# Expert queries, choosing and fetches laid out head by head, with memory work moved among the fetches

## The chip, the core and the metric

The kernel runs on one core of a Trainium2 chip, in one launch. The metric is the device time of one execution in microseconds (us). Engines: PE multiplies matrices (PEld is its weight load), DVE and ACT work on vectors, POOL issues the indirect DMAs that fetch expert rows, SP issues the weight loads.

## What is computed

256 tokens of width 1024 in float32 go through a first mixer (differential attention and retention), a layer of product-key experts, a second mixer (state space and latent attention), an attention over a memory of 256 rows, and a feed-forward layer. The change touches the first two and the memory's keys and values. The expert layer, cut from the reference:

```python
q = (xb @ w_query).reshape(tb, PEER_HEADS, 2, PEER_KEY_DIM // 2)
s = jnp.einsum('thpd,hpnd->thpn', q, sub_keys).astype(jnp.float32)
top_s, top_i = lax.top_k(s, PEER_TOPK)
cand_s = (top_s[:, :, 0, :, None] + top_s[:, :, 1, None, :]).reshape(tb, PEER_HEADS, PEER_TOPK * PEER_TOPK)
...
best_s, pos = lax.top_k(cand_s, PEER_TOPK)
eid = jnp.take_along_axis(cand_i, pos, axis=-1)
gate = jax.nn.softmax(best_s, axis=-1)
u = jnp.take(expert_down, eid, axis=0)
act = jax.nn.gelu(jnp.einsum('thkd,td->thk', u, xb).astype(jnp.float32), approximate=False)
v = jnp.take(expert_up, eid, axis=0)
return jnp.einsum('thk,thkd->td', (gate * act).astype(v.dtype), v)
```

Each token has 8 heads; a head scores 128 keys in each of two halves, takes 16 of each, adds them in pairs, takes the 16 best pairs and so 16 of 16384 experts. For each expert a row of 2048 numbers is fetched: 1024 for a dot product with the token, 1024 that are added to its result with the weight gate times Gelu of the dot.

## The kernel before, in words

A matmul of full precision is made of three (lines 171 to 175): each operand is split into a rounded part and a rest. A piece of weights (line 148, 512 KB) is loaded by SP (`raw`, line 166), rounded by ACT (`wh`, line 167), and its rest taken by DVE (`wl`, line 168); each of the three has three buffers. The framework puts the instructions into each engine's queue from the dependences and a cost of its own, so an engine's order isn't quite that of the program; on an engine they run in that order.

**First mixer.** `mix1` computes six column blocks of `w_in`; three of them (`rqk`, `rv`, `rg`) and then the memory's values and keys are a generator of small steps, `fill`, that is called between the steps of the attentions so that PE has work while DVE and ACT compute softmaxes. The memory has 16 steps (`memory_values`, line 864): eight pieces of `w_mem_v`, with 12 matmuls of 128x512 each, and eight blocks of `w_mem_k`, with 24 of 128x256. Before the change nine of them (eight and one) run in `mix1`. Its results go to DRAM (`memkv`).

**Experts.** Tokens are two tiles of 128. `queries` (line 608) makes 16 blocks of queries, two for each head, and after every fourth block scores two heads of both tiles (line 629) and copies them (line 631). `extract` (line 588) takes the best 16 of a half's 128 scores by five DVE instructions (MAX8, FIND_INDEX8, MATCH_REPLACE8, MAX8, FIND_INDEX8; lines 593 to 605). `choose` (line 634) forms the pairs of the halves, extracts, makes gates, and finds the expert numbers by comparisons and sums (lines 677 to 683) into `eid` (line 685), for four heads at a time. So there are four units of picking: two tiles by two groups of four heads. The first unit ends before the first fetch; the others are laced among the first fetches of tile 0 by `picking`, a generator with a time debt (line 724).

The fetch loop (lines 753 to 794) goes over the 128 expert places of a tile in pairs. A place is an indirect DMA of 1 MB issued by POOL (line 767) into one of eight buffers `uv`, and a dot on DVE (`junk`, line 770). A pair has a Gelu on ACT (line 773), two diagonal tiles on DVE (`dg`, line 779) that carry the weights, and four times two matmul halves on PE (line 783), after which the two buffers are free. The rest of the memory's steps and the picking stand between the pairs of tile 0. After a tile, `joined` (line 816) adds the result to the residual and begins the next mixer's input; its product `xg` (line 828) runs on POOL, in the queue among the fetches of tile 1. The last pieces before the bridge are the latent weights `w_latq`.

The functions that the change touches:

Of the kernel before, what the change touches and what calls it, by code (L numbers as in the profile page):

```python
# [8 lines left out]
F32 = mybir.dt.float32  # L9
# [105 lines left out]
class K:  # L115
# [156 lines left out]
    def proj_N(self, xT, srcs, n, outs, ks=2, k0=0, start=True, stop=True, between=None, mid=None):  # L272
        last = len(srcs) - 1
        for i, s in enumerate(srcs):
            w = self.piece(s, [ks, n], None if i else between)
# [33 lines left out]
    def mix1(self):  # L309
# [3 lines left out]
        with self.tc.tile_pool(name="m1", bufs=1, reuse_waits="tile") as mp:  # L313
# [19 lines left out]
            def block(name):  # L333
                col = {"dq": 0, "dk": 512, "dv": 1024, "rqk": 1536, "rv": 2048, "rg": 2560}[name]
                o = [self.pa([128, 512]) for _ in range(2)]
                for i, _ in enumerate(self.proj_N(hT, [self.rows(I["w_in"], k * 256, 256, col, 512) for k in range(4)], 512, o,
                                     between=(lambda: load_xT(1, 1)) if name == "dq" else None)):
# [3 lines left out]
                if name == "dq":  # L341
                    yield
# [4 lines left out]
                if name == "rg":  # L347
                    gate = nc.scalar.activation(N[name], N[name], AF.Silu)
                    with self.tc.issue_after(gate.ins):
                        self.waves()  # L350
                elif q:
# [146 lines left out]
            fill(2)  # L498
            a = diff_turn(p)
            p = diff_scores(2)  # L500
            w = ret_scores(0)
            fill(2)
            run(norm)
            diff_out(1, a)
# [4 lines left out]
            p = diff_scores(3)  # L509
            fill(2)  # L510
            diff_out(2, a)
            ret_out(1, w)
            w = ret_scores(2)
            fill(2)
            a = diff_turn(p)
            ret_out(2, w)
            w = ret_scores(3)
            fill(1)
            diff_out(3, a)
            ret_out(3, w)  # L520
            ds = ds.rearrange("p t h -> p (t h)")
            nc.vector.tensor_scalar(ds, ds, 1.0 / 128, EPS, op0=OP.mult, op1=OP.add)
            r = self.rsqrt(ds, 8)
            for t in range(2):
# [3 lines left out]
            fill(2)  # L528
            self.to_T([blk(h) for h in range(4)], [dg] * 4, mT[0], mT[1], 0)
            fill(2)  # L530
# [19 lines left out]
            run(half(0, 0))  # L550
            run(half(1, 0))
            self.to_T([blk(4 + h) for h in range(4)], [self.pv("ret_g", h) for h in range(4)], mT[0], mT[1], 4)
            fill(1)
            run(half(0, 4))
# [5 lines left out]
            self.memory = fill  # L560
# [47 lines left out]
    def queries(self, pool, skT, sS):  # L608
# [4 lines left out]
        for b in range(16):  # L613
            if b < 2:
                o = two[b]
            else:
                o = self.pa([128, 256])
                self.proj_T(self.hT, self.piece(I["w_query"][b], [8, 128]), 8, o)
            if b == 2:
                self.r = self.res_r()  # L620
            if b % 4 == 0:
# [1025 lines left out]
```

## Time and profile before

| what | value |
|---|---|
| median of 3 runs | 1355.66 us (1355.19 to 1363.32) |
| the profiled execution | 1354.52 us, span of the profile 1352.6 us |
| busy share PE, PEld, DVE, ACT, POOL | 86, 59, 74, 36, 22% |
| fetched by indirect DMA | 268.45 MB, all DMA 388.07 MB |
| first and last fetch issued | 203.91 and 866.04 us |

The profile is of one execution; its times are from the span's start. A timeline row has start, duration, engine, line, operation, output<-input, and in brackets the idle time before it with the instruction that ended it. A group row has the count, the busy time and mean duration of one, and idle time of the engine before them with what ended it. A window row has the stretch's length, the busy time of each engine with its instructions, the granted TensorE clock as a part of full speed, the busy share of the 16 DMA engines and what they moved.

### The profile page before, as it was taken

Reading aid. Unit: us, or ns where it says so; the run is one execution under the profiler, and the core shown is the slowest. Engines: PE = TensorE matmul, PEld = TensorE weight load, DVE = VectorE, ACT = ScalarE, POOL = GpSimd, SP = SyncE. Lnnn points to the kernel's source line nnn. Section 1 sums busy time; section 2 is a strip of 40 time slices with the busy share of each in tenths; the row PEclk is TensorE's granted clock in tenths of the full one; section 3 lists DMA queues with packets and bytes.
Section 4 is the critical chain, followed back from the end, with each engine's and each line's share of the span. In section 5 each row is a group of like instructions: output and inputs, shape, how many; then the busy total and the mean of one; then the engine's idle time right before and its main releaser. Section 6 shows DMA issues by size and latency. Waiting matters only on the chain.

```text
span 1352.6 us, 16359 instructions
## 1 busy us (share of the span) xinstructions
PE 1158.9 (86%) x5430; PEld 792.1 (59%) x5430; DVE 997.2 (74%) x2334; ACT 489.1 (36%) x969; POOL 291.2 (22%) x280
## 2 busy tenths in 40 slices
PE   8999997668777777787777777789999999999996
PEld 6888996323223222332232222269997898999996
DVE  6877798997666666666656666678996886988887
ACT  6676653210000000100000000056878574755554
POOL 0010104335333334344343343210001000000001
PEclk9999998879999999999999999999999999999999
DMA  7636749899999999899999999936434364556562
GB/s 262 232 120 203 225 150 382 359 352 386 422 422 421 422 421 422 342 423 421 421 421 423 421 422 421 395 101 190 141 106 129 112 231 126 190 187 188 187 185 96
DMA packets 81655, 388.07 MB, mean 287 GB/s; under 512 B 8292, under 2 KB 10404, under 8 KB 48548
## 3 DMA queue, kind: packets, MB, share of 16 engines
q0 software_dynamic: 36864, 268.45, 48.2%
q1 hardware_dynamic: 42692, 115.96, 26.7%
q10 hardware_dynamic: 2016, 2.62, 0.5%
q8 instruction: 43, 0.70, 0.2%
q14 instruction: 40, 0.33, 0.1%
HBM read 383.86 MB, written 3.15 MB: 286 GB/s over the span
## 4 chain that ended last, share of the span: by engine, by line
PE 41%; DMA 23%; issue 13%; DVE 10%; POOL 6%; ACT 1%; POOLq 0%; DVEq 0%; ACTq 0%
DMA uv<-in_uv_dram,eid 23%; POOL uv L767 6%; PE pa L173 6%; PE pa L174 6%; PE pa L175 6%; PE pa L1476 4%; PE pb L173 4%; PE pb L174 4%; PE pb L175 4%; DVE junk L770 2%; DVE wl L168 1%; PE pb L783 1%; PE pb L1060 1%; DVE dg L779 1%; DVE eq L677 1%
## 5 line engine op out<-in xcount | busy, mean ns | idle before, releaser
L783 PE MATMUL pb<-uv,dg 128*128 128x512 f32 x1024 | 486.6, 620 | 168.5 <-DVE dg L779 160.0
L783 PEld LDWEIGHTS pb<-uv,dg 128*128 128x128 f32 x1024 | 190.3, 195 | 460.9 <-DVE dg L779 257.2
L770 DVE SCALAR_TENSOR_TENSOR junk<-uv,xn 128x1024 bf16<-128x1024 f32 x256 | 313.4, 1224 | 166.2 <-DMA uv<-in_uv_dram,eid 159.6
L767 POOL DMA_INDIRECT uv<-in_uv_dram,eid x256 | 260.4, 1017 | 431.7 <-PE pb L783 327.7
L168 DVE TENSOR_TENSOR wl<-raw,wh 128x1024 fp32r<-128x1024 f32 (+3 forms) x203 | 248.8, 1228 | 70.7 <-ACT wh L167 66.8
L167 ACT ACTIVATE wh<-raw 128x1024 fp32r<-128x1024 f32 (+3 forms) x203 | 212.1, 1047 | 196.5 <-PE pa L174 39.5
L773 ACT ACTIVATE dots<-dots,rs_y 128x2 f32<-128x2 f32 x128 | 37.8, 295 | 578.5 <-DVE junk L770 578.1
L173 PE MATMUL pb<-nTh,wh 128*128 128x256 f32 x416 | 117.7, 283 | 0.0
L174 PE MATMUL pb<-nTl,wh 128*128 128x256 f32 x416 | 117.7, 283 | 0.0
L175 PE MATMUL pb<-nTh,wl 128*128 128x256 f32 x416 | 117.4, 283 | 0.0
L779 DVE TENSOR_SCALAR dg<-cvt,dots,gate 128x128 f32<-128x128 f32 x256 | 78.0, 394 | 51.5 <-ACT dots L773 51.5
L174 PEld LDWEIGHTS pb<-nTl,wh 128*128 128x128 f32 x416 | 79.5, 191 | 1.0
L173 PEld LDWEIGHTS pb<-nTh,wh 128*128 128x128 f32 x416 | 79.5, 191 | 1.0
L175 PEld LDWEIGHTS pb<-nTh,wl 128*128 128x128 f32 x416 | 79.5, 191 | 0.0
L173 PE MATMUL pa<-nTh,wh 128*128 128x256 f32 x256 | 74.1, 289 | 0.0
L1500 POOL TENSOR_TENSOR xs<-xr,ng 128x512 f32<-128x512 f32 x4 | 5.1, 1294 | 313.9 <-DVE xr L1498 313.9
L175 PE MATMUL pa<-nTh,wl 128*128 128x256 f32 x256 | 72.5, 283 | 0.0
L174 PE MATMUL pa<-nTl,wh 128*128 128x256 f32 x256 | 72.4, 283 | 0.0
L173 PE MATMUL pa<-wh,nTh 128*128 128x512 f32 (+1 forms) x144 | 58.1, 412 | 8.2 <-ACT wh L167 7.1
L174 PE MATMUL pa<-wl,nTh 128*128 128x512 f32 (+1 forms) x144 | 57.6, 400 | 1.7 <-DVE wl L168 1.6
L175 PE MATMUL pa<-wh,nTl 128*128 128x512 f32 (+1 forms) x144 | 56.7, 394 | 0.0
L173 PEld LDWEIGHTS pa<-nTh,wh 128*128 128x128 f32 x256 | 48.9, 191 | 1.1 <-issue 1.0
(455 smaller groups left out, 1797.5 us busy)
## 6 DMA issues: line engine op xcount, KB each, us to landing
raw<-in_w_ffn_up_dram SPq DMA_DIRECT2D x44, 512.0 KB, 3.6
raw<-in_w_out_dram SPq DMA_DIRECT2D x24, 512.0 KB, 3.7
raw<-in_w_in_dram SPq DMA_DIRECT2D x23, 512.0 KB, 4.7
raw<-in_w_ffn_down_dram SPq DMA_DIRECT2D x22, 512.0 KB, 3.6
raw<-in_w_query_dram SPq DMA_DIRECT2D x16, 512.0 KB, 3.6
raw<-in_w_xbc_dram SPq DMA_DIRECT2D x16, 512.0 KB, 4.3
raw<-in_w_mem_v_dram SPq DMA_DIRECT2D x8, 512.0 KB, 4.7
raw<-in_w_mem_k_dram SPq DMA_DIRECT2D x8, 512.0 KB, 6.2
```

The lines of the kernel that those rows point to most:

```text
L167: nc.scalar.activation(h[:, s], raw[:, s], AF.Copy)
L168: self.wl = nc.vector.tensor_sub(lo[:, s], raw[:, s], h[:, s])
L173: mm(out, a[0], b[0], start=start, stop=False)
L174: mm(out, a[0], b[1], start=False, stop=False)
L175: mm(out, a[1], b[0], start=False, stop=stop)
L677: nc.vector.tensor_tensor(eq, ab[:, s, :, :, None].to_broadcast([128, H, 16, 16]), io, op=OP.is_equal)
L767: nc.gpsimd.indirect_dma_start(x, None, I["uv"], bass.IndirectOffsetOnAxis(ap=eids[:, s + i:s + i + 1], axis=0))
L770: nc.vector.scalar_tensor_tensor(junk, x[:, :1024], 1.0, xn[t], op0=OP.mult, op1=OP.mult, accum_out=dots[:, i:i + 1])
L773: nc.scalar.activation(dots, dots, AF.Gelu, scale=self.r[:, t:t + 1])
L779: nc.vector.tensor_scalar(dg[:, i], self.ident, ds[:, i:i + 1], gates[:, s0 + i:s0 + i + 1], op0=OP.mult, op1=OP.mult)
L783: nc.tensor.matmul(acc[d], dg[:, i], rs[i][:, 1024 + 512 * d:1536 + 512 * d], start=s0 + i == 0, stop=s0 + i == 127)
L1476: nc.tensor.matmul(acc[d][t], a[x][:, t * 128:(t + 1) * 128], w[y][:, d], start=b == 0 and x + y == 0, stop=b == 21 and x == 1)
```

## The change

1. `mix1` has no memory steps among its fillers any more, only the 12 steps of three `w_in` blocks. The order of attention and retention steps is changed, the block `rg` asks for its pieces one ahead, the gate's Silu and the angles come after the differential part, and the memory's normalization is laced into the output projection.
2. Queries are made head by head: two blocks, then that head's scores for both tiles.
3. Picking has seven units instead of four: of tile 0 head 0, head 1, heads 2 and 3, 4 and 5, 6 and 7; of tile 1 two of four heads. `choose` takes the first head and the count.
4. Fetching of tile 0 starts when head 0 is picked. The other query blocks, the picking and all 16 memory steps are laced among the fetches of both tiles.
5. The normalized tokens `xn` are formed by DVE in place of POOL, and the buffers `uv` no longer share space with the keys `skT`.

The diff, cut to its core:

```diff
             def fillers():
                 for name in ("rqk", "rv", "rg"):
                     yield from block(name)
-                yield from self.memory_values(*memory)
             fill = Filler(fillers())
...
             self.show("x1", xr)
-            self.memory = fill
+            self.memory = Filler(self.memory_values(*memory))
...
-        for b in range(16):
...
+        self.r = self.res_r()
+        for h in range(8):
+            qT = pool.tile([128, 2, 256], F32, name="qT", tag="qT", bufs=2)
+            for i in range(2):
+                o = two[i]
+                if h:
+                    o = self.pa([128, 256])
+                    self.proj_T(self.hT, self.piece(I["w_query"][2 * h + i], [8, 128]), 8, o)
+                nc.scalar.activation(qT[:, i], o, AF.Copy)
+                if h and not i:
+                    yield
+            for t in range(2):
+                s = self.pb([128, 2, 128])
...
+                nc.scalar.activation(sS[t][h], s, AF.Copy, scale=self.r[:, t:t + 1])
             yield
...
-            pick = [picks(t, hf) for t in range(2) for hf in range(2)]
+            units = [(0, 0, 1), (0, 1, 1)] + [(0, h, 2) for h in (2, 4, 6)] + [(1, 0, 4), (1, 4, 4)]
+            pick = [(u, picks(*u)) for u in units]
...
+                query = Filler(self.queries(qp, skT, sS))
+                query(4)
+                n = 4
+                picking(1e6, 0, 1)
+                nc.vector.tensor_mul(xn[0], xn[0], self.xr[:, 0])
+                acc = two()
+                tile0 = fetch(0, acc)
+                for s in tile0:
+                    if s in (2, 6, 10) or s > 10 and s % 6 == 4:
+                        query(1)
+                        n += 1
+                    picking(1400, 0, min(8, (n + 1) // 2))
+                    if s in (12, 28):
+                        picking(1e6, 0, 2 if s == 12 else 4)
+                    if n >= 15:
+                        break
+                query.rest()
...
+                for s in tile0:
+                    if s % 6 == 4:
+                        self.memory(1)
+                    picking(1400, 1, 8)
+                    if s in (60, 92):
+                        picking(1e6, 0, 6 if s == 60 else 8)
+                nc.vector.tensor_mul(xn[1], xn[1], self.xr[:, 1])
+                picking(1e6, 1, 4)
...
+                for s in fetch(1, acc):
+                    picking(1400, 1, 8)
+                    if s == 60:
+                        picking(1e6, 1, 8)
+                    if s % 6 == 4 and s < 100:
+                        self.memory(1)
+                    if s == 100:
                         self.memory.rest()
```

What the engines' queues then hold, at three places. `nTh` and `nTl` are the parts of the normalized input of the queries, `memTh` and `memTl` those of the memory, `uv` the fetched rows.

PE, around the first pair of expert matmuls, before:

```order
L175 MATMUL pa<-memTh,wl 128x256
L173 MATMUL pa<-memTh,wh 128x256
L174 MATMUL pa<-memTl,wh 128x256
L175 MATMUL pa<-memTh,wl 128x256
L173 MATMUL pa<-memTh,wh 128x256
L783 MATMUL pb<-uv,dg 128x512 x4
L174 MATMUL pa<-memTl,wh 128x256
L175 MATMUL pa<-memTh,wl 128x256
L173 MATMUL pa<-memTh,wh 128x256
L174 MATMUL pa<-memTl,wh 128x256
L175 MATMUL pa<-memTh,wl 128x256
```

The same place after:

```order
L173 MATMUL pa<-nTh,wh 128x256
L174 MATMUL pa<-nTl,wh 128x256
L175 MATMUL pa<-nTh,wl 128x256
L173 MATMUL pa<-nTh,wh 128x256
L174 MATMUL pa<-nTl,wh 128x256
L175 MATMUL pa<-nTh,wl 128x256
L769 MATMUL pb<-uv,dg 128x512 x4
L629 MATMUL pb<-skT,qT 128x128 x4
L769 MATMUL pb<-uv,dg 128x512 x4
L629 MATMUL pb<-skT,qT 128x128 x4
```

Before, all 16 query blocks and five memory-key blocks stand ahead of the first pair, and the memory's eight value pieces and first key block far ahead of those, in `mix1`. After, 11 query blocks and part of a twelfth stand ahead of it and no memory work; the remaining query blocks, the value pieces and three key blocks follow among the pairs up to the 23rd.

DVE, around the last expert numbers of tile 1 (the last picking of all), before:

```order
L679 TENSOR_TENSOR eq<-eq,rix 128x1024
L779 TENSOR_SCALAR dg<-cvt,dots,gate_1557 128x128 x2
L681 TENSOR_TENSOR eq<-eq 128x64x8
L682 TENSOR_TENSOR eq<-eq 128x64x4
L683 TENSOR_REDUCE rij<-eq 128x64
L770 SCALAR_TENSOR_TENSOR junk,dots<-uv,xn_1569 128x1024
L685 SCALAR_TENSOR_TENSOR eid_1560<-rij 128x64
L770 SCALAR_TENSOR_TENSOR junk,dots<-uv,xn_1569 128x1024
L779 TENSOR_SCALAR dg<-cvt,dots,gate_1557 128x128 x2
L770 SCALAR_TENSOR_TENSOR junk,dots<-uv,xn_1569 128x1024 x2
L779 TENSOR_SCALAR dg<-cvt,dots,gate_1557 128x128 x2
L770 SCALAR_TENSOR_TENSOR junk,dots<-uv,xn_1569 128x1024 x2
```

The same place after:

```order
L756 SCALAR_TENSOR_TENSOR junk,dots<-uv,xn_1380 128x1024
L677 TENSOR_TENSOR eq<-eq,rix 128x1024
L765 TENSOR_SCALAR dg<-cvt,dots,gate_1374 128x128 x2
L679 TENSOR_TENSOR eq<-eq 128x64x8
L680 TENSOR_TENSOR eq<-eq 128x64x4
L681 TENSOR_REDUCE rij<-eq 128x64
L756 SCALAR_TENSOR_TENSOR junk,dots<-uv,xn_1380 128x1024
L683 SCALAR_TENSOR_TENSOR eid_1377<-rij 128x64
L756 SCALAR_TENSOR_TENSOR junk,dots<-uv,xn_1380 128x1024
L765 TENSOR_SCALAR dg<-cvt,dots,gate_1374 128x128 x2
L756 SCALAR_TENSOR_TENSOR junk,dots<-uv,xn_1380 128x1024 x2
L765 TENSOR_SCALAR dg<-cvt,dots,gate_1374 128x128 x2
```

Before, 29 dots of tile 0 stand ahead of the last `eid`; after, 51. After it the queue holds dots and diagonal tiles alone. After the change 35 weight splits (`wl`) from the start of the program stand ahead of the first dot and 20 more between it and the last `eid`; before, 46 and 7.

SP's weight loads, from the first mixer's output weights on, before:

```order
L166 DMA raw<-in_w_mem_v_dram 128x2x512 x8
L166 DMA raw<-in_w_out_dram 128x2x512 x4
L166 DMA raw<-in_w_mem_k_dram 128x1024
L166 DMA raw<-in_w_out_dram 128x2x512 x4
L166 DMA raw<-in_w_query_dram 128x1024 x5
L699 DMA iota<-in_cv_dram 128x16
L708 DMA gf<-in_ffn_gr_dram 128x1024
L710 DMA fgr<-in_final_g_dram 128x1024
L739 DMA skT<-in_skT_dram 128x2048
L166 DMA raw<-in_w_query_dram 128x1024 x11
L166 DMA raw<-in_w_mem_k_dram 128x1024 x7
L166 DMA raw<-in_w_latq_dram 128x864 x4
```

The same place after:

```order
L166 DMA raw<-in_w_out_dram 128x2x512 x8
L166 DMA raw<-in_w_query_dram 128x1024 x5
L699 DMA iota<-in_cv_dram 128x16
L709 DMA xn_1380<-in_ffn_gr_dram 128x1024
L709 DMA xn_1381<-in_ffn_gr_dram 128x1024
L777 DMA skT<-in_skT_dram 128x2048
L166 DMA raw<-in_w_query_dram 128x1024 x11
L166 DMA raw<-in_w_mem_v_dram 128x2x512 x3
L797 DMA fgr<-in_final_g_dram 128x1024
L166 DMA raw<-in_w_mem_v_dram 128x2x512 x5
L166 DMA raw<-in_w_mem_k_dram 128x1024 x8
L166 DMA raw<-in_w_latq_dram 128x864 x4
```

The memory's pieces have moved behind all query pieces; the latent weights (`w_latq`) stand behind them as before. At the change of tiles PE's queue after the change has, between the transposes of tile 0's result and the first pair of tile 1, 31 groups of three matmuls of the memory's keys; before, no memory work is left there.

## Rows read from the trace of the kernel before

**Rows 1.** The page, chain that ended last: share of the span by engine.

```profile
PE 41%; DMA 23%; issue 13%; DVE 10%; POOL 6%; ACT 1%; POOLq 0%; DVEq 0%; ACTq 0%
```

**Rows 2.** Windows by stage: us; PE, PEld, DVE, ACT, POOL busy; granted clock; DMA share; GB/s.

```profile
100.00:150.00 50.00, 50.00 (x271) 42.36 (x270) 37.50 (x81) 32.09 (x61) 0.00 (x0) 1.00 0.60 200
150.00:204.00 54.00, 53.37 (x445) 52.87 (x445) 50.12 (x212) 28.93 (x46) 6.12 (x3) 1.00 0.58 183
400.00:520.00 120.00, 90.25 (x193) 35.16 (x192) 73.73 (x145) 7.09 (x24) 47.32 (x48) 0.99 1.01 422
536.00:600.00 64.00, 50.27 (x121) 22.17 (x122) 39.14 (x81) 8.31 (x27) 26.60 (x26) 0.95 0.94 381
```

**Rows 3.** PE's timeline: start, us, line, operation, end of mix1 and first query block.

```profile
120.02 0.40 PE L173 MATMUL pa<-wh,memTh 128*128 128x512 f32 x1
120.25 0.40 PE L174 MATMUL pa<-wl,memTh 128*128 128x512 f32 x1
...
132.40 0.36 PE L173 MATMUL pa<-memTh,wh 128*128 128x256 f32 x1
...
135.28 0.40 PE L173 MATMUL pa<-wh,mTh 128*128 128x512 f32 x1
...
147.15 0.28 PE L173 MATMUL pa<-nTh,wh 128*128 128x256 f32 x1
```

**Rows 4.** POOL's timeline: the first, eighth, and ninth fetch.

```profile
203.91 1.15 POOL L767 DMA_INDIRECT uv<-in_uv_dram,eid  x1 [43.57 <-DVE vals L602]
...
214.19 1.35 POOL L767 DMA_INDIRECT uv<-in_uv_dram,eid  x1 [0.31 <-issue]
...
226.55 1.26 POOL L767 DMA_INDIRECT uv<-in_uv_dram,eid  x1 [11.01 <-PE pb L783]
```

**Rows 5.** DVE's timeline: an extraction, and the dots of fetches 1, 29, 30, 34 and 52.

```profile
206.57 0.85 DVE L593 MAX8 vals<-sS 128x8 f32<-128x128 f32 x4
...
211.87 1.20 DVE L770 SCALAR_TENSOR_TENSOR junk<-uv,xn 128x1024 bf16<-128x1024 f32 x1
...
310.88 1.22 DVE L770 SCALAR_TENSOR_TENSOR junk<-uv,xn 128x1024 bf16<-128x1024 f32 x1
...
312.16 1.22 DVE L770 SCALAR_TENSOR_TENSOR junk<-uv,xn 128x1024 bf16<-128x1024 f32 x1
...
319.37 1.22 DVE L770 SCALAR_TENSOR_TENSOR junk<-uv,xn 128x1024 bf16<-128x1024 f32 x1 [0.38 <-DMA uv<-in_uv_dram,eid]
...
364.46 1.23 DVE L770 SCALAR_TENSOR_TENSOR junk<-uv,xn 128x1024 bf16<-128x1024 f32 x1 [1.32 <-DMA uv<-in_uv_dram,eid]
```

**Rows 6.** DVE's groups from the first dot to 312 us: busy, mean ns, idle before.

```profile
L770 DVE SCALAR_TENSOR_TENSOR junk<-uv,xn 128x1024 bf16<-128x1024 f32 x29 | 35.2, 1214 | 0.0
...
L779 DVE TENSOR_SCALAR dg<-cvt,dots,gate 128x128 f32<-128x128 f32 x28 | 8.4, 344 | 4.0 <-ACT dots L773 4.0
...
L168 DVE TENSOR_TENSOR wl<-raw,wh 128x1024 fp32r<-128x1024 f32 x4 | 4.8, 1209 | 0.0
...
L168 DVE TENSOR_TENSOR wl<-raw,wh 128x864 fp32r<-128x864 f32 x3 | 3.1, 1042 | 0.0
```

**Rows 7.** The window of that stretch, columns as in rows 2.

```profile
211.87:312.00 100.13, 70.76 (x212) 35.77 (x211) 95.98 (x367) 21.47 (x36) 35.60 (x29) 0.85 0.93 368
```

**Rows 8.** Waits from 204 to 312 us: us in total, times, longest.

```profile
ACT wh L167 <- DMA raw<-in_w_mem_k_dram: 11.6, 3, 5.6
...
DVE dg L779 <- ACT dots L773: 4.0, 2, 3.7
```

**Rows 9.** DMA issues of that stretch: count, KB each, median us to landing.

```profile
raw<-in_w_mem_k_dram SPq DMA_DIRECT2D x3, 512.0 KB, 8.2
```

**Rows 10.** POOL's fetch group, 204 to 312 us.

```profile
L767 POOL DMA_INDIRECT uv<-in_uv_dram,eid x35 | 42.7, 1220 | 109.8 <-DVE vals L602 43.6 <-PE pb L783 40.1 <-DVE idx L596 9.2
```

**Rows 11.** POOL's timeline at the change of tiles.

```profile
548.70 0.94 POOL L767 DMA_INDIRECT uv<-in_uv_dram,eid  x1 [2.36 <-PE pb L783]
560.64 1.27 POOL L828 TENSOR_TENSOR xg<-xr,fgr 128x512 f32<-128x512 f32 x1 [11.00 <-DVE xr L820]
```

More of the change, by code (lines that the diff above doesn't have):

```diff
@@ L497, in mix1 @@
             memory = next(norm)
-            fill(2)
+            fill(1)
             a = diff_turn(p)
             p = diff_scores(2)
+            fill(2)
+            next(norm, None)
+            diff_out(1, a)
             w = ret_scores(0)
-            fill(2)
-            run(norm)
-            diff_out(1, a)
+            a = diff_turn(p)
+            p = diff_scores(3)
+            fill(1)
+            diff_out(2, a)
             ret_out(0, w)
@@ L548, in half @@
                     self.squares(nb)
-            run(half(0, 0))
-            run(half(1, 0))
+            for nb in range(2):
+                for _ in half(nb, 0):
+                    next(norm, None)
+                next(norm, None)
             self.to_T([blk(4 + h) for h in range(4)], [self.pv("ret_g", h) for h in range(4)], mT[0], mT[1], 4)
-            fill(1)
-            run(half(0, 4))
+            for _ in half(0, 4):
+                next(norm, None)
+            run(norm)
             last = half(1, 4)
@@ L733, in picking @@
                         pick.pop(0)
                     else:
[L735 to L746 removed]
+                        debt[0] -= cost
@@ new lines, in fetch @@
+            def fetch(t, acc):
+                gates = self.gate[t].rearrange("p h k -> p (h k)")
+                eids = self.eid[t].rearrange("p h k -> p (h k)")
+                last = None
+                for s in range(0, 130, 2):
+                    new = None
+                    if s < 128:
+                        rows = []
+                        dots = up.tile([128, 2], F32, name="dots", tag="dots", bufs=4)
+                        for i in range(2):
+                            x = up.tile([128, 2048], F32, name="uv", tag="uv", bufs=8)
+                            nc.gpsimd.indirect_dma_start(x, None, I["uv"],
+                                                         bass.IndirectOffsetOnAxis(ap=eids[:, s + i:s + i + 1], axis=0))
+                            junk = self.junk([128, 1024], "junk", BF)
+                            nc.vector.scalar_tensor_tensor(junk, x[:, :1024], 1.0, xn[t], op0=OP.mult, op1=OP.mult,
+                                                           accum_out=dots[:, i:i + 1])
+                            rows.append(x)
+                        nc.scalar.activation(dots, dots, AF.Gelu, scale=self.r[:, t:t + 1])
+                        new = s, rows, dots
+                    if last:
+                        s0, rs, ds = last
+                        dg = up.tile([128, 2, 128], F32, name="dg", tag="dg", bufs=3)
+                        for i in range(2):
+                            nc.vector.tensor_scalar(dg[:, i], self.ident, ds[:, i:i + 1], gates[:, s0 + i:s0 + i + 1],
+                                                    op0=OP.mult, op1=OP.mult)
+                        for i in range(2):
+                            for d in range(2):
+                                nc.tensor.matmul(acc[d], dg[:, i], rs[i][:, 1024 + 512 * d:1536 + 512 * d],
+                                                 start=s0 + i == 0, stop=s0 + i == 127)
+                    last = new
+                    yield s
@@ new lines, in experts @@
+            two = lambda: [self.pb([128, 512]) for _ in range(2)]
+            with self.tc.tile_pool(name="qp", bufs=1, reuse_waits="tile") as qp:
+                skT = qp.tile([128, 16, 128], F32, name="skT")
+                nc.sync.dma_start(skT, I["skT"])
+                query = Filler(self.queries(qp, skT, sS))
[13 more added lines that the diff above has]
+                    if n >= 15:
+                        break
+                query.rest()
```

207 lines of the change are left out of this document (70 added, 137 removed).

## The prediction

> **What bounds the kernel now.** I read the chain of waits first. PE has the largest share, the transfers of the fetched expert rows come second [rows 1]. A share is an average over stages, so the windows by stage come next [rows 2]. From 100 to 150 us PE is busy for 50.00 of 50: mix1 is bound by PE, and a matmul taken out of it shortens it unless that matmul covered a wait. From 150 to 204 us DVE is busy for 50.12 of 54 (splitting query weights and choosing experts), and no fetch runs. From 400 to 520 us the DMA share is 1.01 at 422 GB/s with 48 fetches, so 2.5 us each: there the fetches themselves are the limit. Between these lies a stretch with another limit: from the first dot (211.87 us) to 312 us DVE is busy for 95.98 of 100.13 [rows 7], because the choosing for three of four units is still to be done between 29 dots. Eight fetches fill the buffers by 214.19 us, and the ninth waits for a pair on PE until 226.55 [rows 4]: from there buffers come free at the pace of the dots. Only at 319.37 us does a dot wait for its transfer [rows 5]. So the start is: PE to 147.15 us [rows 3], a DVE-led wait of 56.8 us to the first fetch at 203.91 us [rows 4], DVE again to about 319 us, then the DMA at 2.5 us a fetch. What comes after the last fetch is the same code in both kernels; I carry it over unchanged. The measure of a gain is therefore when dot 52 runs: 364.46 us before, in the DMA-bound part [rows 5].
>
> **Mix1.** Eight memory-value steps and one memory-key block leave it. A value step has 12 matmuls that start 0.23 us apart, 2.8 us; the key block takes 135.28 - 132.40 = 2.88 us [rows 3]. Together 25.2 us of a full PE. What they covered is not in the trace, since PE had no gap. Bounds: nothing lost, or all 25.2 us. The place I see is the chain from the fourth head's output through the reciprocal root and the scaled copies to the transposes, where two fill steps stood after the copies and two after the transposes; of these the first pair, 5.6 us, is the nearest measured cover. I take 5.5 us of stalls: the first query matmul at 147.15 - 25.2 + 5.5 = 127.5 us.
>
> **From there to the first fetch.** In PE's new order the scores of head 0 come after 3.5 query blocks: 3.5 x 2.88 = 10.1 us; scores and copies 2.5 us (estimate). Then DVE has the rows up to the first expert indices. Their price comes from the window of before. Of its 96.1 us (100.13 less 4.0 idle [rows 6, 7]), 29 dots take 32.8 at 1.13 (mean 1.21 less the 0.08 us by which the next instruction begins before the end; the 1.28 us from dot 29 to dot 30 hold a short instruction too [rows 5]), 28 diagonal tiles 7.3 at 0.26, seven splits 7.4; 48.6 us are left for picking. The extraction of four halves runs from 206.57 to about 212.4 us with one split among it, 1.18 us a half [rows 5]; the window has 12 halves, 14.2 us, and three choosings of four heads, so 11.5 us each. Before the first index of the changed kernel stand four halves (4.7), three splits (3.4) and the choosing of head 0 with most of head 1: 7 us (by halves of 11.5/4 it would be 5, as two whole choosings 23; the instructions shrink with the head count, so I stay near the low end). 15.1 us, and 1 us for POOL: 28.7 us in place of 56.8. The first fetch is then at 156.2 us, 47.7 us earlier. Bounds for this step: 24 to 40 us.
>
> **From dot 1 to dot 52.** Dot 1 follows after 8.0 us as before (211.87 - 203.91): 164.2 us. DVE's new order has all picking of both tiles before dot 52, and the splits of 20 pieces of weights. So DVE holds: 52 dots 58.8, 52 diagonal tiles 13.5, 20 splits 22.6, and picking: 27 halves 31.9, the rest of head 1 2, three choosings of two heads at 6.8 (half of 11.5 and 1 us for the fixed part of 34 short instructions; bounds 5.7 and 11.5), two of four heads 23: 77.3. Sum 172.2 us. Idle: in the window of before it was 4.0 us for 29 dots, all behind ACT's Gelu [rows 6, 8]; in proportion 7 us, and 2 more for the two extra exponentials-to-Gelu changes on ACT. I take 9; bounds 0 and 33 (all 11.6 us in which ACT waited for raw weights [rows 8] passed on, for 20 pieces instead of seven). Dot 52 at 164.2 + 172.2 + 9 = 345.4 us, 19.1 us earlier. The DMA would allow more: 52 fetches at 2.5 us and 10.5 MB of raw weights at 422 GB/s are 155 us of the 181. PE has 15 blocks (42 us) and 26 pairs in that time, at 3.76 us a pair (90.25 for 24 [rows 2]) 98 us, and isn't the limit either while its granted clock stays at the 0.85 of that stretch [rows 7].
>
> **What is given back.** (a) In SP's order the latent weights stand behind all memory weights, and two key pieces wait for the change of tiles, so about 3.4 MB that were loaded before 312 us (three of four latent pieces are split there [rows 6]) now fall into the DMA-bound part: 8 us at 422 GB/s, or nothing if they go into the gap at the change of tiles. I take 4. (b) At that change PE now has 31 groups of three key matmuls between the transposes and the first pair of tile 1: 93 x 0.12 = 11 us. The gap was there before: no fetch between 548.70 and 560.64 us because the gated copy stands in POOL's queue [rows 11], and the share over 536 to 600 us is 0.94, some 4 us of DMA lost [rows 2]. Of the 11 us most lies beside five fetches that can still be issued (12.5 us). I take 3.5; bounds 0 and 11. POOL also loses two multiplications before the first fetch, which DVE makes instead (two of about 1.2 us, in the first-fetch wait, beside PE's query blocks): nothing.
>
> **Sum.** -19.1 + 4 + 3.5 = -11.6 us. The profiled execution took 1354.52 us, 1.1 below the median of the runs shown; 1342.9 against the first, 1344 against the second; I give 1343.5. A measurement of this kernel can tell about 1%, that is below 1342.1 or above 1369.2, so this is a gain just at the edge.
>
> **A rule that speaks against the change.** POOL's fetch instruction took 1.22 us on average while DVE was full [rows 10], 0.94 us where DVE waited [rows 11]. 35 fetches in 108 us leave POOL idle most of the time, and 3.5 us a fetch in the new stage would leave it 2.3. The Trainium skill, "SBUF — State Buffer", section "SBUF: two separate sides", says that DVE in its two-port modes keeps GpSimd from writing the descriptors of its own DMAs, and gives 620 ns alone against 3100 ns beside a copy. By that factor of five a fetch would take 4.7 us and POOL would set the pace of the stage; the trace shows a factor of 1.3.
>
> **Rivals.** (A) The DMA decides, not DVE: the choosings in small units cost less than I think, or stalls in mix1 are none. Then the fetches start 47.7 us earlier, and 11 MB more of weights run among them, 26 us at 422 GB/s: -21.7 us, 1333. For it speaks the share of 0.93 that the DMA kept in the window of before [rows 7]; against it that DVE's list there is longer now by 76 us. (B) Slower: weights in the queues. A split on DVE waits for ACT's copy, that for the raw piece, and behind it in DVE's order are dots, diagonal tiles and the choosing; behind those wait PE's pairs, which free the fetch buffers. Pieces took 8.2 us to land among fetches [rows 9], ACT waited up to 5.6 us for one [rows 8], and there are 20 now instead of seven. Three raw buffers hide it if pieces are asked for early (8.2/3 = 2.7 us a piece against 9 us between splits), which speaks against it. If half of the 3.9 us that ACT waited for each of three pieces reaches DVE at each of 20, it is idle for 39 us instead of 9: +18 us, 1373. It turns the gain into none at 21 us of idle time and into a loss over 1% at 34. (C) Mix1 isn't shorter: the memory steps filled PE while the attention chains of DVE and ACT ran (37.50 and 32.09 of 50 us busy [rows 2]). With 25 us of stalls the first fetch is at 176 us, dot 52 at 365, and the 7.5 us given back make it 1362. The full PE speaks for it as much as against it; the reordered steps, with other fills left, against. (D) POOL decides: each fetch is held by three instructions of DVE, 0.94 + 3 x 1.21 = 4.6 us, 1.1 over the 3.5 us that a fetch has: 52 x 1.1 = 57 us, 1400. [rows 10] speak against it.
>
> **How the numbers follow.** Forecast 0.45 (its own range 1334 to 1352), A 0.24, B 0.14, C 0.14, D 0.03. Faster by over 1%: A, and somewhat under half of the forecast's range, 0.42. Slower by over 1%: most of B, and D, 0.14. Within 1%: 0.44. The range goes from 1324 (A without the idle time that I count) to 1368 (C and the beginning of B); outside are B's far end, D, and about 0.05 below.
>
> **What would show it.** In the changed kernel: the first query matmul near 127.5 us (near 147: C); the first fetch near 156; DVE over 90% busy from the first dot to dot 52, that dot near 345 (near 325: A; after 365: B, with DVE's idle time then behind ACT's copies of raw weights); fetch instructions on POOL near 1.2 us (D: over 3.5); then fetches every 2.5 us at 420 GB/s, and between tiles no more than 8 us of lost DMA. My forecast is wrong if the stage up to dot 52 isn't DVE's, or if the change of tiles costs over 10 us.

## The result, and the profile after

The changed kernel takes 1345.18 us (median of 8 runs, 1342.21 to 1348.22) against 1355.67 us of the kernel before beside it: ratio 0.9915, 95% interval 0.9895 to 0.9935, so 10.5 us or 0.8% less. The forecast was 1343.5. The profiled execution is one of the slower of the eight: 1347.02 us, span 1344.9, so 7.5 us under the profiled execution of before; the steps below are read from these two.

The stages after, by windows (columns as in rows 2):

```profile
100.00:127.00 27.00, 26.24 (x127) 21.05 (x125) 22.55 (x55) 17.68 (x35) 0.00 (x0) 1.00 0.45 137
127.00:154.00 27.00, 23.69 (x191) 22.67 (x191) 23.81 (x113) 14.65 (x28) 0.00 (x0) 1.00 0.58 191
220.00:260.00 40.00, 31.98 (x96) 17.50 (x95) 34.87 (x146) 10.77 (x17) 12.95 (x11) 0.91 0.83 309
260.00:312.00 52.00, 44.59 (x122) 23.48 (x121) 48.54 (x189) 11.29 (x18) 19.09 (x15) 0.90 0.88 343
312.00:350.00 38.00, 31.38 (x114) 18.38 (x112) 35.03 (x104) 9.12 (x15) 15.40 (x11) 0.91 1.00 406
400.00:520.00 120.00, 88.95 (x191) 34.58 (x190) 72.65 (x144) 7.09 (x24) 49.17 (x48) 0.99 1.01 422
536.00:600.00 64.00, 55.70 (x225) 33.22 (x224) 38.23 (x76) 13.96 (x36) 28.27 (x23) 0.97 0.92 367
```

PE is no longer without gaps in mix1 (26.24 of 27 us from 100 to 127), and DVE no longer full in the stretch up to 350 us (34.87 of 40 us, then 48.54 of 52), while the DMA share there is 0.83 and 0.88: neither is at its limit from 220 to 312 us. From 400 us on it is the old picture: 48 fetches in 120 us.

The first query matmul on PE (147.15 us before [rows 3]):

```profile
126.36 0.28 PE L173 MATMUL pa<-nTh,wh 128*128 128x256 f32 x1
```

POOL's first and last fetch (203.91 and 866.04 us before; the first is in [rows 4]):

```profile
154.60 1.31 POOL L753 DMA_INDIRECT uv<-in_uv_dram,eid  x1 [69.11 <-PE pa L175]
...
858.72 0.94 POOL L753 DMA_INDIRECT uv<-in_uv_dram,eid  x1 [0.78 <-PE pb L769]
```

DVE's dots 1, 52, 56 and 128 (211.87 and 364.46 us before for the first two [rows 5]):

```profile
162.31 1.23 DVE L756 SCALAR_TENSOR_TENSOR junk<-uv,xn 128x1024 bf16<-128x1024 f32 x1 [3.17 <-DMA uv<-in_uv_dram,eid]
...
349.38 1.22 DVE L756 SCALAR_TENSOR_TENSOR junk<-uv,xn 128x1024 bf16<-128x1024 f32 x1
...
356.75 1.23 DVE L756 SCALAR_TENSOR_TENSOR junk<-uv,xn 128x1024 bf16<-128x1024 f32 x1 [0.66 <-DMA uv<-in_uv_dram,eid]
...
537.59 1.23 DVE L756 SCALAR_TENSOR_TENSOR junk<-uv,xn 128x1024 bf16<-128x1024 f32 x1 [1.32 <-DMA uv<-in_uv_dram,eid]
```

and dots 56 and 128 before, the last being the end of tile 0:

```profile
374.41 1.23 DVE L770 SCALAR_TENSOR_TENSOR junk<-uv,xn 128x1024 bf16<-128x1024 f32 x1 [1.32 <-DMA uv<-in_uv_dram,eid]
...
554.93 1.23 DVE L770 SCALAR_TENSOR_TENSOR junk<-uv,xn 128x1024 bf16<-128x1024 f32 x1 [1.32 <-DMA uv<-in_uv_dram,eid]
```

The query blocks begin 20.8 us earlier, the fetches 49.3 us, dot 52 15.1 us, and the last fetch 7.3 us. The first dot of the fetch-bound part, where dots wait for their transfers, is now dot 56; before it was dot 34. So dot 52 lies ahead of that part after the change and inside it before, and the two are better compared from dot 56 on: there the changed kernel is 17.7 us ahead, and still 17.3 at dot 128. The gain is there in full at the first fetch, about two thirds of it are gone by the fetch-bound part, and 10 us more at the change of tiles and behind it. From the last fetch to the end it is 486.2 us after and 486.6 before.

Between dot 1 and dot 52 (the same window view; before, the stretch of [rows 7] is to be compared):

```profile
162.31:349.38 187.07, 157.44 (x567) 92.67 (x567) 170.62 (x649) 52.50 (x87) 64.22 (x52) 0.92 0.93 368
```

DVE is busy for 170.62 of 187.07 us, idle for 16.45. What it waited for, from 150 to 350 us (total, times, longest; the last line is dot 1's wait, which lies ahead of the stretch):

```profile
DVE dg L765 <- ACT dots L759: 6.9, 5, 3.2
DVE wl L168 <- ACT wh L167: 5.2, 4, 3.0
DVE gs L653 <- ACT ge L652: 3.6, 1, 3.6
DVE junk L756 <- DMA uv<-in_uv_dram,eid: 3.2, 1, 3.2
```

and what ACT waited for ahead of its rounding of raw weights (11.6 us before, for memory keys [rows 8]):

```profile
ACT wh L167 <- DMA raw<-in_w_mem_v_dram: 15.6, 3, 8.1
ACT wh L167 <- DMA raw<-in_w_mem_k_dram: 13.5, 4, 4.7
ACT wh L167 <- DMA raw<-in_w_query_dram: 11.6, 5, 7.2
```

That is 40.7 us of ACT's time, of which DVE sees a part: directly as waits for `wh`, and, as I read the order of ACT's queue, through the Gelu and exponential that stand behind a blocked rounding. SP, which loads the pieces, waits in turn for DVE's splits to free a `raw` buffer (its queue's waits over the same 200 us):

```profile
SPq L166 <- DVE wl L168: 156.4, 21, 35.3
```

POOL's fetch instruction, from 154 to 350 us and from 400 to 520 us ([rows 10] has it before; the bracket at the end is idle time):

```profile
L753 POOL DMA_INDIRECT uv<-in_uv_dram,eid x57 | 71.2, 1248 | 193.5 <-PE pa L175 69.4 <-PE pb L769 55.0 <-DVE eq L680 12.8
```

```profile
L753 POOL DMA_INDIRECT uv<-in_uv_dram,eid x48 | 49.2, 1024 | 71.9 <-PE pb L769 64.5 <-DVE junk L756 4.5 <-DVE dg L765 2.3
```

At the change of tiles SP now loads the last latent weights:

```profile
550.66 13.47 SPq L166 DMA_DIRECT2D raw<-in_w_latq_dram  x3
575.80 3.12 SPq L166 DMA_DIRECT2D raw<-in_w_latkv_dram  x2
```

and the DMA moves, from 530 to 620 us (packets, MB, share of 16 engines):

```profile
q0 software_dynamic: 4262, 31.03, 84.3%
q1 hardware_dynamic: 1008, 2.67, 7.7%
q10 hardware_dynamic: 720, 0.66, 2.2%
```

against this in the kernel before, where there was no weight load in these 90 us:

```profile
q0 software_dynamic: 4842, 35.29, 95.8%
```

The fetches get 4.26 MB less, 3.33 MB of it taken by weights and memory writes (7.9 us at 422 GB/s), and the rest is 0.93 MB or 2.2 us of idle transfer. Together that is 10.1 us. Fetch 129 is 16.6 us earlier than before, fetch 160 only 7.4.

### The profile page after: what moved, and what is told of

Same layout as the page of the kernel before. It is cut to its first block, busy times and chain, and to the rows that moved or that the text cites. A ratio compares the mean times of both kernels' runs of the same rounds, so it can differ in the third digit from the quotient of the medians.

```text
span 1344.9 us, 16416 instructions
## 1 busy us (share of the span) xinstructions
PE 1161.5 (86%) x5430; PEld 794.0 (59%) x5430; DVE 1000.5 (74%) x2417; ACT 495.6 (37%) x984; POOL 298.9 (22%) x278
## 4 chain that ended last, share of the span: by engine, by line
PE 38%; DMA 28%; DVE 12%; issue 12%; POOL 6%; ACT 3%; POOLq 0%; SPq 0%; DVEq 0%; ACTq 0%
DMA uv<-in_uv_dram,eid 22%; POOL uv L753 5%; PE pa L173 5%; PE pa L174 5%; PE pa L175 5%; PE pa L1503 4%; PE pb L173 4%; PE pb L174 4%; PE pb L175 4%; DVE wl L168 3%; PE pb L769 2%; DVE junk L756 2%; DMA raw<-in_w_in_dram 2%; DMA raw<-in_w_mem_v_dram 1%; DMA raw<-in_w_mem_k_dram 1%
## 5 line engine op out<-in xcount | busy, mean ns | idle before, releaser
L753 POOL DMA_INDIRECT uv<-in_uv_dram,eid x256 | 272.8, 1066 | 487.4 <-PE pb L769 317.7
L175 PEld LDWEIGHTS pa<-nTh,wl 128*128 128x128 f32 x256 | 48.7, 191 | 5.3 <-DVE wl L168 5.1
```

The costliest lines, as they stand in the source:

```text
L175: mm(out, a[1], b[0], start=False, stop=stop)
L753: nc.gpsimd.indirect_dma_start(x, None, I["uv"], bass.IndirectOffsetOnAxis(ap=eids[:, s + i:s + i + 1], axis=0))
```

## The experiments

All medians below stand beside runs of the kernel before on the same chip (1355.35 to 1356.48 us in the four sets).

| kernel | median us | ratio, 95% interval | first fetch | dot 52 | last fetch |
|---|---|---|---|---|---|
| before | 1355.67 | 1 | 203.91 | 364.46 | 866.04 |
| after | 1345.18 | 0.9915 (0.9895 to 0.9935) | 154.60 | 349.38 | 858.72 |
| e1: after, picking tied | 1326.52 | 0.9775 (0.9754 to 0.9796) | 156.86 | 323.35 | 838.71 |
| e2: after, memory in tile 0 | 1347.38 | 0.9936 (0.9919 to 0.9953) | 157.24 | 353.38 | 853.02 |
| e3: mix1 of before | 1343.61 | 0.9909 (0.9890 to 0.9927) | 171.59 | 352.91 | 855.16 |
| e4: experts of before | 1344.23 | 0.9911 (0.9893 to 0.9928) | 185.60 | 353.20 | 854.42 |
| f1: before, picking tied | 1346.38 | 0.9928 (0.9910 to 0.9947) | 204.12 | 352.50 | 857.18 |
| f2: e3, picking tied | 1328.73 | 0.9802 (0.9785 to 0.9819) | 173.29 | 333.29 | 839.96 |
| f3: e1 with e2 | 1324.03 | 0.9771 (0.9751 to 0.9790) | 155.75 | 329.73 | 836.38 |
| f4: f3, gated copy on DVE | 1326.14 | 0.9775 (0.9759 to 0.9792) | 158.48 | 332.07 | 837.90 |
| g1: after, no memory splits | 1329.40 | 0.9801 (0.9774 to 0.9828) | 154.81 | 330.22 | 840.20 |
| g2: after, no memory bytes | 1329.25 | 0.9798 (0.9773 to 0.9822) | 154.60 | 333.61 | 840.55 |
| h1: e4, picking tied | 1339.57 | 0.9871 (0.9851 to 0.9891) | 186.12 | 347.23 | 851.62 |

**Each half of the change alone (e3, e4).** e3 takes the function `mix1` of before into the changed kernel; e4 takes `queries`, `choose` and `experts` of before into it.

e3:

> The first mixer of before (nine memory steps in it) with the expert layer of the change. DVE theory: first fetch at about 175 us (20.8 us of mix1 lost, the head by head start kept), three splits fewer in the stage, dot 52 at about 360, nothing given back at the change of tiles: 4 to 5 us faster than before, 1351. Rival (all of the gain comes from the head by head start): 28 us earlier and kept, 1335 or lower. Bytes rival: 28 us earlier less 15 for 6.3 MB, 1342.

e4:

> The first mixer of the change (no memory steps) with the expert layer of before (all 16 memory steps in it). DVE theory: first fetch at about 183 us, nine splits and 10 us more on DVE and 5 us more of waits before picking ends (dot 34 instead of 29), dot 34 at about 313 us instead of 319: 5 to 6 us faster than before, 1350. Rival (shortening mix1 is the whole gain): 20 us earlier less 11 us for 4.7 MB, 1345, as fast as the whole change.

Both halves are as fast as the whole. My theory's sums came out 6 to 7 us too slow for either. The rivals that count bytes were nearer: 1342 for e3 and 1345 for e4. The reading of e4's rival, that mix1 is the whole gain, is excluded by e3, which has the mix1 of before and the same time. From the start of the program to dot 52, the windows of the whole, of e3 and of e4:

```profile
0.00:349.38 349.38, 306.40 (x1410) 217.42 (x1411) 300.11 (x1023) 157.06 (x294) 77.97 (x65) 0.96 0.77 287
```

```profile
0.00:352.91 352.91, 313.29 (x1527) 229.80 (x1528) 305.63 (x1027) 163.12 (x304) 78.37 (x64) 0.97 0.79 289
```

```profile
0.00:353.20 353.20, 315.96 (x1531) 230.18 (x1532) 299.05 (x944) 156.08 (x289) 85.50 (x67) 0.97 0.77 288
```

DVE has 299 to 306 us of work up to dot 52 in each, and 47 to 54 us idle. The fetches start at 154.6, 171.6 and 185.6 us, and dot 52 comes at 349.4, 352.9 and 353.2. From dot 1 to dot 52, e3 and then e4:

```profile
178.61:352.91 174.30, 145.70 (x605) 88.29 (x604) 166.77 (x645) 48.01 (x85) 66.51 (x51) 0.95 0.96 374
```

```profile
193.56:353.20 159.64, 133.96 (x454) 74.66 (x453) 139.56 (x444) 36.69 (x62) 66.34 (x51) 0.95 1.00 407
```

e3 is like the whole: DVE is busy for 166.77 of 174.30 us. In the sum for it I had kept 16 us of idle time; it had 7.5, with fewer weights among the fetches. e4 isn't: its DMA share is 1.00 and DVE is idle for 20 us, and its dots wait for transfers from dot 42 on. So DVE's list holds the whole and e3 up to dot 52, but e4 mostly waits for bytes.

**Picking out of the way (e1, f1).** In the changed kernel and in the kernel before every picking instruction is put behind the last dot that was traced (below: tied):

```diff
...
-                    cost = next(pick[0][1], None)
+                    if self.dot is None:
+                        cost = next(pick[0][1], None)
+                    else:
+                        with self.tc.issue_after(self.dot.ins):
+                            cost = next(pick[0][1], None)
...
-                            nc.vector.scalar_tensor_tensor(junk, x[:, :1024], 1.0, xn[t], op0=OP.mult, op1=OP.mult,
+                            self.dot = nc.vector.scalar_tensor_tensor(junk, x[:, :1024], 1.0, xn[t], op0=OP.mult, op1=OP.mult,
```

e1:

> The changed kernel, with every picking instruction put behind the dot of its own pair in DVE's queue, so that picking is spread over tile 0 (last expert numbers at dot 126 in place of 51). DVE theory (the stretch up to dot 52 is set by DVE's list of 170 us): about 45 us of picking leave that list, dot 52 comes at 318 to 325 us in place of 349, where the DMA limit takes over, and the time falls by 20 to 25 us, to about 1322. Rival, bytes (the earlier start is eaten by 11 MB of weights that now run among the fetches): the DMA has no room left, dot 52 moves by under 8 us and the time by under 5. Second rival: fetches starve on late expert numbers, POOL waits for them, time above 1345.

f1:

> The kernel before, with its picking tied behind the dots (last expert numbers at dot 86 in place of 29), nothing else of the change. DVE theory: what bounds the stretch before catching up in both kernels is picking; without it the fetches run at 2.5 us from dot 1 (211.9 us), dot 52 at 350 in place of 364.5: 13 to 15 us faster than before, 1341, as fast as the change and 15 us slower than the change tied in the same way (1326.5). Rival (tying pays only together with the early start): under 5 us, 1352.

e1 is 18.7 us faster than the whole change, a little under the 20 to 25 expected, with dot 52 at 323.35 us inside the range given; the bytes rival's 5 us are excluded. f1 gains 9 us with nothing of the change (13 to 15 expected; dot 52 at 352.5, 350 expected). Dots 6, 42 and 52 of e1, its window from dot 1 to dot 52, and that from 350 to 400 us:

```profile
180.96 1.22 DVE L761 SCALAR_TENSOR_TENSOR junk<-uv,xn 128x1024 bf16<-128x1024 f32 x1 [0.37 <-DMA uv<-in_uv_dram,eid]
...
298.22 1.23 DVE L761 SCALAR_TENSOR_TENSOR junk<-uv,xn 128x1024 bf16<-128x1024 f32 x1 [1.53 <-DMA uv<-in_uv_dram,eid]
...
323.35 1.23 DVE L761 SCALAR_TENSOR_TENSOR junk<-uv,xn 128x1024 bf16<-128x1024 f32 x1 [1.32 <-DMA uv<-in_uv_dram,eid]
```

```profile
163.34:323.35 160.01, 145.35 (x554) 87.24 (x553) 127.44 (x373) 44.59 (x80) 58.90 (x53) 0.97 1.02 419
350.00:400.00 50.00, 37.50 (x79) 14.64 (x78) 44.52 (x166) 5.75 (x13) 22.66 (x20) 0.97 1.01 420
```

Dots 1, 2 and 6 wait for their transfers, dots 7 to 41 don't, and from dot 42 on many do; but the DMA share is 1.02 with 419 GB/s over the whole stretch, where the untied kernel has 0.93 and 368. DVE has 127.44 us of work in that stretch in place of 170.62; the picking now runs later (44.52 us busy from 350 to 400, where the untied kernel has 32.85). Of the 26.0 us by which dot 52 is earlier than in the untied kernel 20.0 are left at the last fetch. Of the other 6, 2.6 are gone by dot 56 (333.28 against 356.75 us), because dot 52 of the untied kernel isn't yet in the fetch-bound part, and 3.7 more by dot 128 (517.85 against 537.59). In that last part no weights are loaded in either kernel, and e1's mean is 413 GB/s in place of 421; it falls to 328 from 430 to 440 us, where picking is still going on and DVE is busy for 9.34 of 10 us.

f1's window from dot 1 to dot 52 shows the same limit:

```profile
211.91:352.50 140.59, 109.19 (x290) 50.15 (x289) 117.93 (x394) 20.20 (x42) 58.57 (x50) 0.93 1.02 420
```

**The two halves again, with picking tied (f2, h1).**

f2:

> The first mixer of before with the expert layer of the change and tied picking. With DVE's list out of the way the DMA's bytes are the limit from the first fetch on: the fetch starts 15 us later than in e1 (171 against 156.9 us) and 4.7 MB less of weights run among the fetches (11 us); the loss at the change of tiles (8 us) goes too. Bytes theory for this regime: 1322 to 1326, no slower than e1. Rival (an earlier start is kept whole once DVE has room): 15 us slower than e1, 1341.

h1:

> The first mixer of the change (no memory steps) with the expert layer of before and tied picking: the fourth of the tied pairs (f1, f2, e1). Bytes theory for the tied kernels: against f1 the first fetch comes 18 us earlier (185.6) and 4.7 MB more of memory weights run among the fetches, 11 us: 7 us faster than f1, 1339. If shortening mix1 is worth what it was between f2 and e1 (2 us): 1344. If an earlier first fetch is kept whole once picking is tied: 1328.

With the tie the four kernels are 1346.4 (neither half), 1339.6 (mix1), 1328.7 (experts) and 1326.5 us (both). For h1 the byte count gave 1339 and met it. For f2 it gave 1322 to 1326, 3 us too fast, and the rival's 1341 is far off. So once DVE's list is spread the order of the halves shows: the new expert layer (head by head fetching with its finer picking) is worth 13 to 18 us, shortening mix1 2 to 7.

Where the rest of an earlier start goes can be counted from the DMA's side. What it moved from the first fetch to the last, before, after, in e3 and in e4:

```profile
DMA packets 38833, 269.70 MB, mean 407 GB/s; under 512 B 4302, under 2 KB 5454, under 8 KB 6606
```

```profile
DMA packets 43560, 282.10 MB, mean 401 GB/s; under 512 B 4719, under 2 KB 5999, under 8 KB 11247
```

```profile
DMA packets 40633, 276.52 MB, mean 405 GB/s; under 512 B 4504, under 2 KB 5656, under 8 KB 8344
```

```profile
DMA packets 41395, 275.84 MB, mean 412 GB/s; under 512 B 4532, under 2 KB 5812, under 8 KB 9140
```

At the 422 GB/s of the stretch from 400 to 520 us these bytes have a time, and the rest is transfer time that went unused. It is a second count of the same time: DVE's work and waits count the way to dot 52, bytes and unused transfer that to the last fetch.

| kernel | first to last fetch us | MB | us at 422 GB/s | rest us |
|---|---|---|---|---|
| before | 662.1 | 269.7 | 639.1 | 23.0 |
| after | 704.1 | 282.1 | 668.5 | 35.6 |
| e3 | 683.6 | 276.5 | 655.3 | 28.3 |
| e4 | 668.8 | 275.8 | 653.6 | 15.2 |
| f1 (before, tied) | 653.1 | 269.8 | 639.4 | 13.7 |
| e1 (after, tied) | 681.9 | 281.0 | 665.9 | 16.0 |
| f2 (e3, tied) | 666.7 | 275.1 | 651.9 | 14.8 |
| h1 (e4, tied) | 665.5 | 275.5 | 652.9 | 12.6 |

With picking tied the rest is 13 to 16 us in all four, so among them it is mostly the start and the bytes that differ: of the 16 to 18 us by which a short mix1 brings the first fetch forward, 13.5 to 14.0 go into the bytes that then run among the fetches. Untied, the whole change starts 49.3 us earlier, spends 29.4 of them on 12.4 MB more and 12.6 on unused transfer time, and keeps 7.3. e3 starts 32.3 us earlier, spends 16.2 and 5.3, and keeps 10.9; e4 starts 18.3 us earlier, spends 14.5 on bytes, and even uses the DMA 7.8 us better than before. Tying gives the whole change 18.7 us, e3 14.9, the kernel before 9.0, and e4 4.7: most where the rest was large.

**DVE's list or the bytes (g1, g2).** In the untied changed kernel, for the memory's 16 pieces alone (`self.mem` is set while a memory step runs): g1 leaves out the split on DVE, g2 the load.

```diff
 # g1
-        lo = t("wl", F32R)
+        lo = h if getattr(self, "mem", False) else t("wl", F32R)
...
-            self.wl = nc.vector.tensor_sub(lo[:, s], raw[:, s], h[:, s])
+            if lo is not h:
+                self.wl = nc.vector.tensor_sub(lo[:, s], raw[:, s], h[:, s])
 # g2
-            self.raw = nc.sync.dma_start(raw[:, s], src[:, s])
+            if getattr(self, "mem", False):
+                raw = self.xr[:, 0]
...
+            else:
+                self.raw = nc.sync.dma_start(raw[:, s], src[:, s])
```

g1:

> The changed kernel, untied, with the 16 memory pieces loaded, rounded and multiplied as before, but their rest isn't formed on DVE (the rounded part stands for it in the third matmul, so keys and values of the memory are wrong by that). All bytes stay; 14 splits of 1.13 us leave DVE's list ahead of dot 52, and picking ends at dot 42. DVE theory: dot 52 16 to 21 us earlier, at 328 to 333, the time 1327 to 1331. Bytes rival: nothing changes, 1345.

g2:

> The changed kernel, untied, with the 16 memory pieces taken from a tile that is in SBUF in place of a load of 8.4 MB (so keys and values of the memory are wrong); rounding, splits and matmuls stay, three splits come after dot 52 instead of ahead of it. Bytes rival: the 14 pieces ahead of dot 52 are 7.3 MB, 17 us at 422 GB/s: dot 52 at 332, the time 20 us lower at 1325. DVE theory: dot 52 earlier by the three splits (3.4 us) and by what DVE idled for raw weights (5 us of 16), at 339 to 342; behind it the last pieces no longer take 6 us of the DMA: 1330 to 1335.

g1 keeps all bytes and gains 15.8 us; dot 52 at 330.22, as the DVE theory had it. The bytes rival had no change. g1 from dot 1 to dot 52:

```profile
161.68:330.22 168.54, 151.27 (x575) 90.37 (x575) 155.71 (x635) 52.76 (x87) 55.14 (x52) 0.96 0.99 400
```

g2's time (1329.25) lies between the two forecasts, and dot 52 (333.61) at the rival's figure. The windows tell which it is: from dot 1 to dot 52, and two inside it:

```profile
161.23:333.61 172.38, 149.53 (x573) 89.49 (x573) 167.15 (x645) 49.45 (x84) 62.22 (x51) 0.97 0.93 358
200.00:250.00 50.00, 46.59 (x174) 27.42 (x174) 50.00 (x207) 17.04 (x27) 17.48 (x15) 1.00 0.94 363
250.00:300.00 50.00, 41.70 (x120) 22.34 (x119) 50.00 (x193) 10.44 (x18) 19.34 (x16) 0.97 0.82 307
```

The DMA isn't at its limit there (0.94 and 0.82, 363 and 307 GB/s), and wasn't with the loads (0.83 and 0.88 from 220 to 312 us in the changed kernel), and DVE is busy for all of 100 us. So up to dot 52 it isn't for lack of transfer time that the loads cost; they cost DVE's waits: its idle time from dot 1 to dot 52 falls from 16.45 to 5.23 us, and its work by 3.5 us, the three splits that come later. I had expected that only 5 of the 16 hang on raw weights; 11 do. Whether a piece is late because it lands late or because SP waits for a free `raw` buffer before it loads it, no run tells apart.

**The change of tiles (e2, f3, f4).** e2 and f3 call the memory steps at every second pair of tile 0 in place of every third; f4 forms `xg` on DVE as well.

```diff
-                    if s % 6 == 4:
+                    if s % 4 == 0:
                         self.memory(1)
...
-        nc.gpsimd.tensor_mul(self.xg[t], xr[:, t, c], self.fg[:, c])
+        nc.vector.tensor_mul(self.xg[t], xr[:, t, c], self.fg[:, c])
```

e2:

> The changed kernel, with a memory step at every second pair of tile 0 in place of every third, so that no memory block is left at the change of tiles and the latent weights load early. DVE theory: four more splits before dot 52, 5 us later there, but the 8 us that are given back at the change of tiles go: a gain of 1 to 3 us, 1343. Rival (the eleven us of key matmuls on PE at the change are the whole loss and the stage has room): gain of 7 us, 1338.

f3:

> e1 and e2 together: picking tied, a memory step at every second pair, none left at the change of tiles. If the 8 us given back at the change are the key blocks and the late latent weights there, this is 5 to 8 us faster than e1: 1320. Rival (the bytes only move; what is loaded earlier delays fetches by as much): within 2 us of e1, 1326.

f4:

> f3 with the gated copy at the change of tiles on DVE in place of POOL, so that fetches 132 to 136 don't queue behind it. If that gap (11 us without a fetch in every kernel so far) costs the 4 to 6 us of DMA time that the share shows, 4 us faster than f3: 1316. Rival (buffers, not the copy, hold the fetches there): same as f3.

In e2's profile dot 52 is 4.0 us later (5 expected), and the last fetch 5.7 us earlier: from dot 52 to the last fetch it is 499.6 us, against 509.3 in the changed kernel and 501.6 before, so what was given back at the change of tiles is gone. The times don't show it: the profiled execution (1341.09 us) is the fastest of seven that go up to 1348.81, and the median is 1347.38. Whether e2 gains anything stays open. f3 is 2.5 us under e1, with intervals that overlap, nearer to the rival's 1326 than to 1320: what is loaded earlier delays fetches by nearly as much (dot 52 6.4 us later than in e1). f4 isn't faster than f3. POOL's timeline at the change, f3 and then f4:

```profile
518.66 0.94 POOL L758 DMA_INDIRECT uv<-in_uv_dram,eid  x1 [1.76 <-PE pb L774]
529.90 1.27 POOL L857 TENSOR_TENSOR xg<-xr,fgr 128x512 f32<-128x512 f32 x1 [10.31 <-issue]
```

```profile
532.90 1.13 POOL L758 DMA_INDIRECT uv<-in_uv_dram,eid  x1 [0.78 <-PE pb L774]
546.39 0.98 POOL L758 DMA_INDIRECT uv<-in_uv_dram,eid  x1 [12.36 <-DVE dg L770]
```

In f3 the gap of 11 us ends with the gated copy as in [rows 11]; in f4 there is no copy, five more fetches are issued, the last of them the eighth of tile 1 (there are eight buffers), and the next waits 12.36 us, which a diagonal tile on DVE ends. The gap moves. Buffers hold the fetches there, not the copy.

## Why the prediction was right

The stage up to dot 52 is DVE's, as forecast: busy for 91% of it, and e1 and g1, which take work off its list, bring dot 52 forward by 26.0 and 19.2 us. That is the mechanism, and it is shown. The closeness of the time, 1345.18 against 1343.5 us, is partly luck: in the two profiled executions, from which every step is read, the gain is 7.5 us of the 11.6 in the sum. The profiled execution of before is 1.2 us under its median and that of after 1.8 over, and the medians are 10.5 apart.

Point by point, forecast and measured. **Mix1**: 5.5 us of stalls for 25.2 us taken out; 4.4 (25.2 less the 20.8 by which the queries begin earlier). **To the first fetch**: 28.7 us; 28.2, of two parts that miss by 2 us or more each, one up and one down. The first extraction of head 0 comes 14.7 us after the first query matmul in place of 12.6 (the 2.5 us in it for scores and copies rested on no row), and the first fetch 13.6 us after that in place of 16.1:

```profile
141.03 0.49 DVE L595 MAX8 vals<-sS 128x8 f32<-128x128 f32 x2 [2.49 <-ACT sS L630]
```

**DVE's list from dot 1 to dot 52**: 172.2 us; 170.6. **Its idle time**: 9 us; 16.45, the one term of that sum that was off. I took the row on Gelu waits as the nearest and passed on little of the row on raw weights [rows 8]; g2 shows that 11 of the 16 us are raw weights, so that row was the nearer. Dot 52 came at 349.4 in place of 345.4: -15.1 us, not -19.1. But dot 52 is no measure of the gain after the change, since the fetch-bound part begins four dots later; at dot 56 it is -17.7 us, so the error is smaller than it looks. **Given back**: 7.5 us; 7.8 counted from dot 52 (15.1 less 7.3), but 10.0 from dot 128, the end of tile 0, to the last fetch (17.3 less 7.3). Neither the sum nor its parts were right: I took 4 us for late weights and 3.5 for the key matmuls at the change, and the rows show about 8 us of weights and memory writes and 2 of idle transfer. That is at the edge of the 10 us that I had named as a sign of being wrong. f4 shows besides that the gap at the change, which I laid to the copy in POOL's queue, is the buffers'.

**Rivals.** A (the DMA decides): not up to dot 52, where the share is 0.93 and where g1 gains 15.8 us with all bytes kept. But the price that it names is paid: 12.4 MB more among the fetches, 29.4 us (A had 11 MB and 26 us), and my sum, which goes by DVE's list, doesn't show it. B (raw weights in the queues): its mechanism is there, in 11 of DVE's 16 us of idle time; at 21 us of idle time it would have eaten the gain. C (mix1 not shorter): no. D (POOL decides): no; a fetch instruction took 1.25 us against 1.02 in the fetch-bound part. The Trainium skill, "SBUF — State Buffer", section "SBUF: two separate sides", says that descriptor writing waits while DVE holds the shared port, and gives 620 ns alone against 3100 ns beside a copy, a factor of five. The rows have 1.2 for POOL's instruction, beside DVE instructions of many kinds, which doesn't tell apart port and other causes; a factor of five isn't seen here.

What the prediction didn't say, and the runs show, is how little of the change was needed. I treated the two halves as parts of one chain whose gains add up. They don't: 12 us each, 10.5 together. With the new expert layer an earlier start runs into DVE's list (the whole, e3), and with the new mix1 alone it goes mostly into bytes (e4).

## What to carry to other kernels

When work is started earlier, ask which engine's total work has to be done by the point where the next limit takes over: here DVE had 300 us to do by dot 52, and starting fetches 49 us earlier moved that point by 15. Count too what else will then share the limiting resource: 29 of the 49 us went into bytes, mostly weights that used to be loaded while no fetch ran. The gain came when work that isn't due yet was held back in the full engine's queue (1326.5 us with picking tied, 1324.0 with the memory's steps nearer together as well, against 1345.2): a scheduler that fills gaps brings it forward, so tie it to something late. Read a queue's order for work that stands far ahead of its use.

## What was not expected of the hardware

Weight loads among the fetches didn't lower the DMA's total: 419 GB/s in e1 with splits and queries laced in, as against 422 with fetches alone. Up to dot 52 of the untied kernel they cost by being late instead: without the 8.4 MB of memory pieces (g2) DVE idles 11 us less, while the DMA's mean goes down from 368 to 358 GB/s. A 512 KB piece of the memory landed after 8.4 us (values) and 10.3 us (keys) beside the fetches, as medians; the query pieces of the kernel before, from 100 to 200 us and without fetches, landed after 3.6 us.
